# A rank scatter on one core: four-tile loads with four buffers and 9 directly copied tiles, in place of two-tile loads with eight buffers and 11

## The chip, the core and the metric

The kernel runs on one core of one Trainium2 chip. The metric is the device time of one launch in microseconds (us); the other cores do nothing. The core has five engines that run side by side: PE (TensorE, matrix products), DVE (VectorE), ACT (ScalarE), POOL (GpSimd) and SP (SyncE). Data moves by DMA: an engine's instruction stream issues a transfer, and 16 DMA engines, shared by everything the core issues, carry it out. A transfer that covers 128 partitions is cut into packets that are spread evenly over the 16 DMA engines, and each of them adds 1 to the transfer's semaphore when its own share has landed, so a transfer is done when its semaphore has risen by 16.

## The reference

```python
def setup_inputs():
    B, N, D = 8, 2048, 2560
    return {"x": randn(B, N, D) as float32, "scores": randn(B, N) as float32}

def reference(x, scores):
    order = np.argsort(scores, axis=1)
    ranks = np.argsort(order, axis=1)
    out = np.zeros_like(x)
    out[b_idx, ranks, :] = x
    return out
```

In each of 8 batches, row n of `x` (2560 floats, 10 KB) goes to the row of `out` that is the rank of its score among the batch's 2048 scores. So 16384 rows of 10 KB, 167.8 MB, are read once and written once, in an order that depends on the data.

## The kernel before

A tile is 128 rows of one batch (1.31 MB); there are 16 tiles in each batch, 128 in all. Two things go on at once.

**Ranks.** DVE finds the rank of every row. For a batch it first copies all 2048 scores, which PE has spread over the 128 partitions, from PSUM into `s_all` (L235). Then for each tile it counts how many scores are smaller than each of the tile's 128 own scores (the instructions of L258, two counts and one product with the triangular `mask` that settles equal scores inside a group), adds the counts (L284, L290) and turns them into integers (L307). The product is over a whole group of tiles, so its width is 128 times the number of tiles in the group.

**Moving the rows.** `GROUPS` (L56) cuts a batch into groups of tiles. An entry (first row, m, batches) stands for m tiles; in the batches named last it is moved directly, in the others through SBUF. `ORDER` (L57) is the order of groups in a batch; it fixes the order of the ranks and of the transfers.

- *Bulk groups* (list `BULK`, numbered k over all batches) are loaded into one of `NBUF` buffers `xb` by one DMA, `load` (L119 to L125, issued at L122): partition p gets m consecutive rows, m times 10 KB in one piece. Then m indirect DMAs, `scatter` (L358 to L369, issued at L361), each send 128 rows of 10 KB to the rows named by `rank_i`. Load 0 is issued by SP, all other loads and all scatters by POOL, in one ring which each DMA engine works off in order.
- *Direct groups* go from DRAM to DRAM without a buffer. SP and ACT take turns of 16 rows (L326 to L344): they read 16 row addresses from `rows_i` into registers and issue one DMA for each row, split over the 16 DMA engines into packets of 640 bytes. These wait only for the ranks of their own group.

The order of POOL's work is the loop at L373. `LAG` is 2: before step k sends its scatters, POOL waits until the scatters of step k-2 have wholly landed, and issues into their buffer the load of step k+NBUF-2. Then it waits for load k and for the ranks of group k (L381, L382), and issues the scatters of step k. So at the moment at which the wait for the scatters of step k-2 ends, the ring holds exactly the load of step k+NBUF-3 (the one issued a step ago) and, behind it, the scatters of step k-1. At the start POOL issues NBUF-1 loads in a row (L371, L372).

```python
        for k, (b, g) in enumerate(BULK):
            if k >= LAG and k + NBUF - LAG < len(BULK):
                scatters_done(pl, k - LAG)
                load(pl, k + NBUF - LAG, s_load[(k - LAG) % NBUF])
            ... wait for load k and the ranks of (b, g) ...
            for j in range(GROUPS[g][1]):
                scatter(k, j, 0, P, rank_i, s_scat[i][j])
```

Before, the groups are: tile 0 of each batch, direct in all 8 batches; tile 1, direct in batches 0 to 2 and bulk in the others; and seven groups of two tiles, all bulk. That makes 11 direct tiles (1408 rows), and 61 bulk loads: 56 of two tiles and 5 of one, 117 tiles and 117 scatters in all. Eight buffers of 20 KB per partition hold them.

SP and ACT wait for their own row copies at L348; SP waits for the last NBUF steps' scatters at L394.

Of the kernel before, what the change touches and what calls it, by code (L numbers as in the profile page):

```python
# [7 lines left out]
P = 128  # L8
# [32 lines left out]
def kernel(  # L41
# [7 lines left out]
    B, N, D = x.shape  # L49
# [3 lines left out]

    GROUPS = [(0, 1, range(B)), (P, 1, range(3))] + [(256 * i, 2, ()) for i in range(1, 8)]  # L56
    ORDER = [2, 0, 1, 3, 4, 5, 6, 7, 8]  # L57
    MMAX = max(m for _, m, _ in GROUPS)
    MDIR = max([m for _, m, direct in GROUPS if direct], default=1)
    MBULK = max(m for _, m, direct in GROUPS if len(direct) < B)  # L60
    BULK = [(b, g) for b in range(B) for g in ORDER if b not in GROUPS[g][2]]
    DIRECT = [(b, g) for b in range(B) for g in ORDER if b in GROUPS[g][2]]

    SPLIT = ()
    LAST = 2
    NBUF = 8
    LAG = 2
    G = 16

    def first_col(g):  # L70
        return GROUPS[g][0] // P

# [14 lines left out]
    rows_i = [pool.tile([MDIR, P], I32, name=f"rows_i{i}") for i in range(len(DIRECT))]  # L87
    xb = [pool.tile([P, MBULK * D], F32, name=f"x{i}") for i in range(NBUF)]
    ps_col = psum.tile([P, 512], F32, name="ps_col")
# [8 lines left out]
    with tc.tile_critical(no_gpsimd_drain=True):  # L98
# [6 lines left out]
        s_first = nc.alloc_semaphore("first")  # L105
        s_load = [nc.alloc_semaphore(f"load{i}") for i in range(NBUF)]
        s_scat = [
            [nc.alloc_semaphore(f"scat{i}_{j}") for j in range(MBULK)]
            for i in range(NBUF)
        ]  # L110
        s_rows = {sp: nc.alloc_semaphore("rows_sp"), act: nc.alloc_semaphore("rows_act")}
        s_last = [
            [nc.alloc_semaphore(f"last{i}_{j}") for j in range(MBULK)]
            for i in range(NBUF)
        ]
        n_scat = [[0] * MBULK for _ in range(NBUF)]
        n_last = [[0] * MBULK for _ in range(NBUF)]

# [111 lines left out]
        for b in range(B):  # L230
# [11 lines left out]
            dve.after(dve, t_copied)  # L242
            for g in ORDER:
                r, m, _ = GROUPS[g]
# [128 lines left out]
        for k, (b, g) in enumerate(BULK):  # L373
            i = k % NBUF
# [50 lines left out]
```

## Time and profile before

| | |
|---|---|
| median of 3 runs | 795.35 us (795.24, 795.35, 797.09) |
| the profiled execution, its own time | 797.09 us |
| span of its profile, first to last instruction | 795.4 us |
| DVE busy | 411.2 us (52% of the span) |
| POOL busy | 148.4 us (19%) |
| PE busy | 33.3 us (4%) |
| HBM read, written | 167.84 MB, 167.77 MB: 422 GB/s over the span |
| row copies issued by SP and by ACT | 704 each, from 24.3 us to 690.5 us |
| loads issued by POOL | 60, from 2.7 us to 734.9 us |
| scatters issued by POOL | 117, from 17.8 us to 753.1 us |

The profile's times count from the first instruction. Busy time leaves out the issuing of DMAs by SP and ACT and counts POOL's. In the view of stretches each line gives a stretch's ends and length, then for PE, PE's weight load, DVE and POOL the busy time and number of instructions, then the granted PE clock, then the mean busy share of the 16 DMA engines and the GB/s that they moved. A byte copied from DRAM to DRAM counts once in these GB/s, a byte that goes through SBUF twice. In the timeline each line gives start, duration, engine, line, operation, what is written from what, and in brackets how long the engine was idle before and what ended that. The trace also holds every DMA packet with its start, duration, bytes and queue, and every semaphore increment with its time.

### The profile page before, as it was taken

Reading aid. Unit: us, or ns where it says so; the run is one execution under the profiler, and the core shown is the slowest. Engines: PE = TensorE matmul, PEld = TensorE weight load, DVE = VectorE, ACT = ScalarE, POOL = GpSimd, SP = SyncE. Lnnn points to the kernel's source line nnn. Section 1 sums busy time; section 2 is a strip of 40 time slices with the busy share of each in tenths; the row PEclk is TensorE's granted clock in tenths of the full one; section 3 lists DMA queues with packets and bytes.
Section 4 is the critical chain, followed back from the end, with each engine's and each line's share of the span. In section 5 each row is a group of like instructions: output and inputs, shape, how many; then the busy total and the mean of one; then the engine's idle time right before and its main releaser. Section 6 shows DMA issues by size and latency. Waiting matters only on the chain.

```text
span 795.4 us, 4586 instructions
## 1 busy us (share of the span) xinstructions
PE 33.3 (4%) x155; PEld 27.2 (3%) x155; DVE 411.2 (52%) x1002; POOL 148.4 (19%) x186
## 2 busy tenths in 40 slices
PE   3002010020020100200000000000000000000000
PEld 3001010010010100100000000000000000000000
DVE  6999999999999999999994000000000000000000
POOL 3102121212121212022111212122121212111600
PEclk9555555555555555555555555555555555555555
DMA  8999999999999999999999999999999999999994
GB/s 364 431 402 365 424 415 425 417 422 417 425 417 418 347 420 422 422 367 420 421 420 423 397 397 421 420 419 380 420 411 423 420 386 407 401 431 426 390 428 193
DMA packets 70737, 321.57 MB, mean 404 GB/s; under 512 B 25384, under 2 KB 47912, under 8 KB 47912
## 3 DMA queue, kind: packets, MB, share of 16 engines
q0 software_dynamic: 25488, 304.10, 91.3%
q1 hardware_dynamic: 22688, 9.94, 4.9%
q10 hardware_dynamic: 22528, 7.25, 3.9%
q14 instruction: 32, 0.26, 0.1%
q8 instruction: 1, 0.02, 0.0%
HBM read 167.84 MB, written 167.77 MB: 422 GB/s over the span
## 4 chain that ended last, share of the span: by engine, by line
DVE 47%; DMA 40%; issue 4%; POOL 3%; PE 1%; POOLq 0%; SPq 0%
DVE trash L258 41%; DMA out_dram<-x,rank_i 38%; DVE s_all L235 2%; DMA x<-in_x_dram 2%; POOL out_dram L361 2%; DVE rank L284 1%; DVE rank L290 1%; DVE rank_i L307 1%; POOL x L122 1%; DMA s_in<-in_scores_dram 0%; PE ps_all L190 0%; PE ps_col L169 0%; DVE rows_i L220 0%; POOLq L28 0%; DVE s_col L177 0%
## 5 line engine op out<-in xcount | busy, mean ns | idle before, releaser
L258 DVE TENSOR_SCALAR_CACHE_REDUCE trash<-s_all,s_col 128x1792 bf16<-128x1792 f32 (+9 forms) x248 | 315.3, 1306 | 0.3
L122 POOL DMA_DIRECT2D x<-in_x_dram x60 | 33.8, 565 | 545.8 <-DMA out_dram<-x,rank_i 376.5
L361 POOL DMA_INDIRECT out_dram<-x,rank_i x117 | 112.8, 964 | 59.0 <-issue 35.3
L258 DVE SCALAR_TENSOR_TENSOR trash<-s_all,s_col,mask 128x256 bf16<-128x256 f32 (+1 forms) x128 | 59.0, 461 | 0.0
L190 PE MATMUL ps_all<-ident,s_col 128*128 128x128 f32 x128 | 27.2, 399 | 247.4 <-DVE s_all L235 247.0
L190 PEld LDWEIGHTS ps_all<-ident,s_col 128*128 128x128 f32 x128 | 24.4, 213 | 249.4 <-DVE s_all L235 249.0
L235 DVE COPY s_all<-ps_all 128x512 f32<-128x512 f32 x32 | 20.1, 683 | 1.8 <-PE ps_all L190 1.5
L258 DVE DVE_READ_ACCUMULATOR trash<-s_all,s_col 128x1 f32 x248 | 19.9, 80 | 0.0
L290 DVE TENSOR_TENSOR rank<-rank,acc 128x2 f32<-128x2 f32 (+1 forms) x72 | 11.5, 160 | 2.5
L284 DVE TENSOR_TENSOR rank<-acc,acc 128x2 f32<-128x2 f32 (+1 forms) x72 | 11.5, 160 | 2.5
L307 DVE CAST rank_i<-rank 128x2 int32<-128x2 f32 (+1 forms) x61 | 10.7, 176 | 1.8
L258 DVE DVE_READ_ACCUMULATOR trash<-s_all,s_col,mask 128x1 f32 x128 | 10.2, 80 | 0.0
L300 PE MATMUL ps_row<-ident,rank 128*1 128x128 f32 x11 | 4.1, 372 | 101.3 <-DVE rank L290 92.7
L300 PEld LDWEIGHTS ps_row<-ident,rank 128*1 128x1 f32 x11 | 0.9, 79 | 105.0 <-DVE rank L290 95.5
L220 DVE TENSOR_SCALAR rows_i<-ps_row 1x128 int32<-1x128 f32 x11 | 3.0, 272 | 0.0
L177 DVE COPY s_col<-ps_col 128x128 f32<-128x128 f32 x1 | 0.3, 292 | 4.8 <-PE ps_col L169 4.8
L169 PE MATMUL ps_col<-ident,s_in 8*128 8x8 f32 x16 | 2.0, 261 | 4.0 <-DMA s_in<-in_scores_dram 4.0
L169 PEld LDWEIGHTS ps_col<-ident,s_in 8*128 8x128 f32 x16 | 1.9, 211 | 4.0 <-DMA s_in<-in_scores_dram 4.0
L150 POOL TENSOR_SCALAR_AFFINE_SELECT mask<-mask 128x256 f32<-128x256 f32 x2 | 0.8, 398 | 0.0
L162 DVE MEMSET acc<- 128x128 f32 x1 | 0.2, 165 | 1.1 <-SPq L98 1.1
L133 POOL MEMSET mask<- 128x512 f32 x1 | 0.5, 525 | 0.0
L132 POOL MEMSET ident<- 128x128 f32 x1 | 0.2, 204 | 0.5 <-SPq L98 0.5
(5 smaller groups left out, 0.7 us busy)
## 6 DMA issues: line engine op xcount, KB each, us to landing
x<-in_x_dram POOLq DMA_DIRECT2D x55, 2560.0 KB, 19.2
out_dram<-in_x_dram SPq DMA_DIRECT2D x704, 10.0 KB
out_dram<-in_x_dram ACTq DMA_DIRECT2D x704, 10.0 KB
x<-in_x_dram POOLq DMA_DIRECT2D x5, 1280.0 KB, 16.7
x<-in_x_dram SPq DMA_DIRECT2D x1, 2560.0 KB, 13.4
out_dram<-x,rank_i POOLq DMA_INDIRECT x117, 23.5
s_in<-in_scores_dram SPq DMA_DIRECT2D x1, 64.0 KB
```

The lines of the kernel that those rows point to most:

```text
L122: line.eng.dma_start(out=xb[k % NBUF][:, :m * D], in_=x[b, r:r + P * m, :].rearrange("(p j) d -> p (j d)", j=m),).then_inc(sem, 16)
L150: nc.gpsimd.affine_select(out=part, in_=part, pattern=[[0, MMAX], [-1, P]], compare_op=OP.is_ge, fill=0.0, base=-half, channel_multiplier=1,)
L169: nc.tensor.transpose(out=ps_col[:, B * c:B * (c + 1)], in_=s_in[:, r + j:r + m * P:m], identity=ident[:B, :B],)
L190: nc.tensor.transpose(out=ps_all[:, P * c:P * (c + 1)], in_=s_col[:, c, b:b + 1].to_broadcast([P, P]), identity=ident[:],)
L220: nc.vector.tensor_scalar(out=rows_i[DIRECT.index((b, g))][:m, :], in0=ps_row[:m, :P], scalar1=float(b * N), scalar2=float(ROW), op0=OP.ad ...
L235: nc.vector.tensor_copy(out=s_all[:, 512 * q:512 * (q + 1)], in_=ps_all[:, 512 * q:512 * (q + 1)],)
L258: how.pop("do")(out=trash[i][:, :P * (hi_c - lo_c)], in0=s_all[:, P * lo_c:P * hi_c], accum_out=acc[which][:, col:col + 1], **how,)
L284: nc.vector.tensor_tensor(out=rank[:, cols], in0=acc[0][:, cols], in1=acc[1][:, cols], op=OP.add)
L290: nc.vector.tensor_tensor(out=rank[:, cols], in0=rank[:, cols], in1=acc[2][:, cols], op=OP.add)
L300: nc.tensor.transpose(out=ps_row[:m, :P], in_=rank[:, cols], identity=ident[:])
L307: nc.vector.tensor_copy(out=rank_i[:, cols], in_=rank[:, cols])
L361: nc.gpsimd.indirect_dma_start(out=out_flat, out_offset=bass.IndirectOffsetOnAxis(ap=index[:hi - lo, col:col + 1], axis=0), in_=xb[k % NBU ...
```

## The change

```diff
-    GROUPS = [(0, 1, range(B)), (P, 1, range(3))] + [(256 * i, 2, ()) for i in range(1, 8)]
-    ORDER = [2, 0, 1, 3, 4, 5, 6, 7, 8]
+    GROUPS = [(0, 1, range(B)), (P, 1, range(1))] + [(256 + 512 * i, 4, ()) for i in range(3)] + [(1792, 2, ())]
+    ORDER = [2, 0, 1, 3, 4, 5]
...
-    NBUF = 8
+    NBUF = 4
```

Tile 1 of a batch is now direct in batch 0 alone, so 9 tiles (1152 rows) are copied directly and 119 go through SBUF. The other 14 tiles of a batch are three groups of four tiles and one of two. That makes 39 bulk loads: 24 of four tiles (40 KB per partition, 5.2 MB), 8 of two and 7 of one. There are four buffers of 40 KB per partition, the same 160 KB as before. `MMAX` rises from 2 to 4, so `mask` is twice as wide and the products with it in a group of four tiles cover 512 columns. Everything else follows from these three constants: POOL issues 38 loads and 119 scatters, three loads ahead at the start instead of seven, and at step k the load of step k+2 instead of k+6; SP and ACT copy 576 rows each. The order in a batch is: four tiles, one (tile 1, where it is bulk), four, four, two. Who issues what, and the waits, stay as they are.

## Prediction

> **What bounds the kernel now.** I read the page's slices and queues first.
>
> ```profile
> DMA  8999999999999999999999999999999999999994
> ...
> q0 software_dynamic: 25488, 304.10, 91.3%
> q1 hardware_dynamic: 22688, 9.94, 4.9%
> q10 hardware_dynamic: 22528, 7.25, 3.9%
> ```
>
> The DMA engines are busy in every slice but the first and last, and POOL's ring (q0) takes nine tenths of their time; q1 (SP) and q10 (ACT) are the row copies. No compute engine is near. So the time is the bill of packets, plus whatever holds the engines up. The stretches show where that is:
>
> ```profile
> 10.00:46.00 36.00, 2.71 (x18) 1.88 (x18) 35.44 (x86) 3.90 (x4) 0.58 1.01 431
> 66.00:80.00 14.00, 1.25 (x5) 0.26 (x3) 13.76 (x33) 3.31 (x4) 0.62 1.03 343
> 100.00:250.00 150.00, 12.38 (x52) 10.14 (x52) 147.43 (x358) 28.78 (x35) 0.51 1.02 420
> 262.00:275.00 13.00, 3.18 (x15) 3.18 (x16) 12.72 (x33) 4.21 (x6) 0.50 1.03 308
> 340.00:352.00 12.00, 0.00 (x0) 0.00 (x0) 11.79 (x31) 3.21 (x5) 0.50 1.04 345
> 740.00:780.00 40.00, 0.00 (x0) 0.00 (x0) 0.00 (x0) 9.10 (x10) 0.50 1.01 417
> 786.00:791.00 5.00, 0.00 (x0) 0.00 (x0) 0.00 (x0) 0.00 (x0) 0.50 0.06 25
> ```
>
> Steady work moves 420 GB/s; at 66, 262 and 340 us it falls to 343, 308 and 345 while the busy share stays above 1. There the ring has run dry on some engines, which do row copies alone, or the packets take longer. And the last line: 0.06 is one sixteenth. In the last 5 us one DMA engine works alone. The semaphore increments say the same: the 16 engines' shares of one DMA land 1.5 us apart in the first loads, 4 to 5 us at 100 us, up to 9.3 us at 350 us, and the last scatter 7 us apart. So the end is set by one late engine; what the other 15 lose costs nothing unless it slows that one. POOL's timeline shows why the ring runs dry:
>
> ```profile
> 31.32 0.95 POOL L361 DMA_INDIRECT out_dram<-x,rank_i  x1 [0.30 <-issue]
> 63.73 0.57 POOL L122 DMA_DIRECT2D x<-in_x_dram  x1 [31.46 <-DMA out_dram<-x,rank_i]
> ...
> 70.42 0.56 POOL L122 DMA_DIRECT2D x<-in_x_dram  x1 [3.58 <-DMA out_dram<-x,rank_i]
> ...
> 87.49 0.57 POOL L122 DMA_DIRECT2D x<-in_x_dram  x1 [13.98 <-DVE rank L284]
> ...
> 261.90 0.57 POOL L122 DMA_DIRECT2D x<-in_x_dram  x1 [10.49 <-DMA out_dram<-x,rank_i]
> ...
> 272.58 0.56 POOL L122 DMA_DIRECT2D x<-in_x_dram  x1 [7.58 <-DMA out_dram<-x,rank_i]
> ...
> 287.48 0.56 POOL L122 DMA_DIRECT2D x<-in_x_dram  x1 [11.81 <-DVE trash L258]
> ```
>
> At 63.73 step 2 gets past the wait for step 0's scatters, and only step 1's two scatters are left in the ring (two tiles, 6.2 us), less what the quick engines have already done. The load issued at 261.90 starts its first packet at 265.5, 3.6 us after its issue. So if the late engine has less than its lag plus 3.6 us queued when POOL wakes, quick engines run dry. (The 13.98 us named after DVE end when step 2's scatters have landed, at 86.9; DVE is ahead of POOL by then.)
>
> **The bill of packets.** In the trace's packet records the usual durations are 0.385 us for 10 KB, 0.761 for 20 KB, 0.032 for 640 bytes and 0.009 for a semaphore packet; the next packet starts 0.004 (after the semaphore one 0.003) before the last ends, so the spacings are 0.381, 0.757, 0.028 and 0.006. 10 KB more cost 0.376, so I estimate a 40 KB packet, which this trace does not hold, at 0.757 + 0.752 = 1.509; bounds: 0.757 twice (1.514) and four times 0.376 (1.504), half a us either way over the 192 on an engine. Each engine carries 8 packets and one semaphore packet of every load and scatter, and one 640-byte and one semaphore packet of every row.
>
> Before, per engine: 448 x 0.757 = 339.1 and 40 x 0.381 = 15.2 for loads, 936 x 0.381 = 356.6 for scatters, 177 x 0.006 = 1.1, rows 1408 x 0.034 = 47.9; sum 759.9. After: 192 x 1.509 = 289.7, 64 x 0.757 = 48.4, 56 x 0.381 = 21.3, scatters 952 x 0.381 = 362.7, 157 x 0.006 = 0.9, rows 1152 x 0.034 = 39.2; sum 762.2. **Term 1: +2.3 us**: the two tiles cost more through SBUF than directly, and longer packets save little.
>
> **What the late engine loses besides.** From its first load packet (2.5 us) to its last landing (790.9) are 788.4 us, 28.5 above the bill. Taking each DMA's last increment minus that of the DMA before, less its bill and 0.034 us for each packet of the ring (one packet of q1 and one of q10 are served between two of q0): load 8, issued at 63.73, takes 10.42 us where 6.36 are due, 4.1 lost; load 7, 1.2. Ten steps in batches 3 to 7 meet a one-tile group, so only three tiles' worth (9.2 us) is queued at the wake; loads around them lose 1.8 (load 23), 0.7 (load 28) and 0.3 to 0.6 several times, together about 5, so 0.5 each. About 3.5 are lost in five lumps of 0.7 at instruction fetches (8 KB packets on another queue). Scatter packets of the late engine are lengthened to about 0.41: 450 such records, 12.0 us above 0.385. 2.7 stay unassigned.
>
> **What the change does to these.** *Start.* Step 2 now wakes with step 1's four scatters queued, 12.4 us against a need of 3.6 plus some 5 of lag: the 4.1 of load 8 go. Does the first scatter come in time? The 14 tiles loaded ahead take 14 x 8 x 0.3765 = 42 us from 2.5, so until 46 with rows. DVE has four tiles' ranks at about 23.5 (10.58, then 3.1 a tile from its timeline, plus 0.26 for each 512-wide product, estimated from 0.346 at 128 and 0.477 at 256 columns); load 0, on SP's queue, has 12 us of packets and shares engines with POOL's loads, landing by 27 at the latest. Step 1's ranks come at about 44, before its scatters are due at 59. **Term 2: -4.1.** If that cover is gone (a load 0 20 us late), DMA idles for what is missing.
>
> *Wakes with little queued.* The groups run 4, 1, 4, 4, 2. At step k the ring holds load k+1 and scatters k-1: in tiles 3, 8, 5, 6, 8 through a batch. Only the first step of batches 1 to 7 has three. Ten such wakes become seven; everything else has more than before. At 0.5 each: 3.5 in place of 5. **Term 3: -1.5**; bounds for one wake: 0 (load 31 lost nothing) and 4.1 (load 8). I take the mean of the ten, which have the same three tiles queued.
>
> *Fetches* scale with the unrolled rows, 18% fewer: **term 4: -0.6.** *Lengthened scatter packets:* they come only while rows are copied (none after 700.2 us). The share of scatter packets in the ring's rises from 16/27 to 32/45, rows fall to 1152: 834 against 819 of them meet rows. Nothing; bounds -2.2 (18%, if the rows cause them) and +0.2.
>
> *Costed at nothing.* DVE: 96 products wider, +25 us, 24 fewer group endings of 0.5, so it ends near 430 instead of 415, while batch b's ranks are due at some 99 x b. POOL's wider mask (memset 0.53, selects 2 x 0.40, doubled) delays its first load by 1.3 us behind load 0's 12. Rows: 576 of a queue take two turns each, 1152 of the ring's 1413, so they end near 650 and SP's last waits follow as before; at three turns each (1728) they would become the end. The tail after the last landing stays 4.5 us.
>
> The sum: 2.3 - 4.1 - 1.5 - 0.6 = -3.9. The profiled execution (797.09, of it 795.4 span) would become 793.2; the median of the runs, 1.7 below it, 795.35 - 3.9 = **791.4**.
>
> **Two rules.** The Trainium skill (DMA: Bandwidth & Descriptors, Anatomy of one DMA) adds about 2.0 us to each DMA beside its bytes; 22 fewer loads would save 44 us if they ran one by one, giving 751. Here the trace disagrees: behind a DMA's semaphore packet the next one's data follows after 0.006 us. The same page (Latency and other measured facts) guesses that slow DMA engines suffer from the descriptor ring's port; with 11% fewer ring packets (1593 to 1413) that would be an estimated 1.3 of the 12.0 us, 790.1. The scatter-only stretch from 740 us, all ring and no rows, has none of it, which speaks against.
>
> **Rivals.** *The wakes become the bound (slower).* Place: step 4, 9, ... 34, where POOL waits for a four-tile scatter and quick engines sit dry, then all read a 5.2 MB load in step. Price per wake p: the total is -7.4 + 7p, so it decides from p = 1.06. With load 23's 1.8: +5.2, 800.6. For: loads read in step after a dry moment took 1 to 2 us per 20 KB packet. Against: nine of ten such wakes cost under 0.8. *No change:* load 8's 4.1 come from the start of scatters under row copies, not from the short ring, and return: +0.2, 795.6. For: load 7 lost 1.2 with a full ring. Against: the dip to 343 GB/s comes 3 us after the wake. *More gained:* long runs of one kind of packet free the late engine of its lengthened ones: -3.9 - 12.0, 779.5; nothing but the two pure stretches speaks for it.
>
> **How the numbers follow.** Forecast 0.46, no change 0.25, slower 0.23, more gained 0.06. The runs can't tell less than 0.3% (2.4 us) from nothing. The forecast and the large gain give faster 0.52. p = 0 gives 788.0, the low end; the high end, 798, takes in the no-change case and p up to 1.4. The likeliest one's own range is 788 to 793.
>
> **What would show it.** Packets of 40 KB at 1.51 us; load 4 (issued near 60 us) in 12.4 us on the late engine; seven dips a hundred us apart; row copies ended near 650; one engine last at the end. Wrong if 40 KB packets run over 1.55, if DMA idles before 60 us, or if rows run past 780.

## The result, and the profile after

The changed kernel takes 803.49 us (median of 4 runs, 802.98 to 804.12); the kernel before, in the same comparison, 795.91. The ratio is 1.0094 (95% interval 1.0076 to 1.0111): 7.6 us slower, where 3.9 us faster was forecast. The span of the profile grew from 795.4 to 801.9 us, by 6.5; the profiled run of before was the longest of its four, hence the difference.

The page of the changed kernel, slices and queues:

```profile
DMA  9999999999999999999999999999999999989993
...
q0 software_dynamic: 22608, 306.72, 90.7%
q1 hardware_dynamic: 18592, 11.24, 5.1%
q10 hardware_dynamic: 18432, 5.94, 3.1%
```

The DMA engines are as full as before, with POOL's ring at nine tenths. The stretches of the changed kernel (columns as in the view of before), the first where load 8 had cost the kernel before its dip, the next in steady work, four around the wakes with three tiles queued, and the end:

```profile
66.00:80.00 14.00, 2.06 (x10) 1.65 (x8) 13.86 (x32) 5.16 (x6) 0.62 1.05 437
100.00:200.00 100.00, 8.09 (x34) 6.71 (x34) 98.86 (x216) 17.92 (x20) 0.52 1.02 421
206.00:220.00 14.00, 0.00 (x0) 0.00 (x0) 13.90 (x32) 5.44 (x7) 0.50 1.06 256
310.00:324.00 14.00, 0.00 (x0) 0.00 (x0) 13.86 (x32) 4.01 (x5) 0.50 1.05 425
611.00:625.00 14.00, 0.00 (x0) 0.00 (x0) 0.00 (x0) 5.92 (x7) 0.50 1.04 388
712.00:724.00 12.00, 0.00 (x0) 0.00 (x0) 0.00 (x0) 3.96 (x5) 0.50 0.98 385
789.00:794.00 5.00, 0.00 (x0) 0.00 (x0) 0.00 (x0) 0.00 (x0) 0.50 0.15 66
795.50:801.90 6.40, 0.00 (x0) 0.00 (x0) 0.00 (x0) 0.00 (x0) 0.50 0.00 0
```

The dip at 66 us is gone (437 GB/s against 343), as forecast. There are new ones at three of the four wakes with three tiles queued, down to 256 GB/s; the one at 310 us moves 425. One late engine still ends the transfers (0.15 is mostly one sixteenth in a stretch that begins with several). The last line is the surprise: after the last landing, at 794.7 us, the core does nothing that the profile counts for 7.2 us. Before, it was 4.1 us (from the last semaphore increment at 791.3; the prediction's 790.9 and 4.5 count from the end of the last data packet). The waits of SP's queue say for what, in the kernel before

```profile
SPq L420 <- PEq L420: 3.3, 2, 2.9
```

and in the changed one

```profile
SPq L420 <- PEq L420: 6.4, 2, 6.0
```

(line waited at, releaser, us in total, times, longest us). This is the barrier at the end of the program. PE is only the last to report; the instruction records, which the page doesn't count as busy, show that all engines wait for one instruction of POOL, a drain:

```
kernel    start us  duration us  engine  instruction
before      791.64        3.015  POOL    DRAIN
changed     795.08        6.112  POOL    DRAIN
```

So the sum comes out as follows, with the bill recomputed from the counted packets by the spacings of the prediction, and the late engine's loss as what its last landing lies above the bill:

| | before | changed | difference |
|---|---|---|---|
| first load packet, us | 2.6 | 2.5 | -0.1 |
| bill of packets | 759.9 | 762.3 | +2.4 |
| loss of the late DMA engine | 28.7 | 29.8 | +1.1 |
| last landing at | 791.3 | 794.7 | +3.4 |
| from there to the end of the span | 4.1 | 7.2 | +3.1 |

These differences add up to the 6.5 us of the span. The prediction had +2.3 for the bill, -6.2 for the late engine's loss (terms 2 to 4) and nothing for what follows the last landing.

### The profile page after: what moved, and what is told of

The parts are those of the page before. It is cut to its first block, busy times and chain, and to the rows that moved or that the text cites. A ratio compares the mean times of both kernels' runs of the same rounds, so it can differ in the third digit from the quotient of the medians.

```text
span 801.9 us, 3940 instructions
## 1 busy us (share of the span) xinstructions
PE 33.0 (4%) x153; PEld 27.3 (3%) x153; DVE 425.9 (53%) x930; POOL 141.5 (18%) x166
## 4 chain that ended last, share of the span: by engine, by line
DMA 73%; issue 12%; POOL 10%; POOLq 0%; SPq 0%
DMA out_dram<-x,rank_i 68%; POOL out_dram L361 9%; DMA x<-in_x_dram 6%; POOL x L122 1%; POOLq L28 0%; SPq L128 0%; SPq L420 0%; SPq L98 0%
## 5 line engine op out<-in xcount | busy, mean ns | idle before, releaser
L258 DVE TENSOR_SCALAR_CACHE_REDUCE trash<-s_all,s_col 128x768 bf16<-128x768 f32 (+6 forms) x248 | 315.1, 1305 | 0.3
L361 POOL DMA_INDIRECT out_dram<-x,rank_i x119 | 117.2, 985 | 80.4 <-issue 36.5
L122 POOL DMA_DIRECT2D x<-in_x_dram x38 | 21.5, 567 | 543.9 <-DMA out_dram<-x,rank_i 354.2
L258 DVE SCALAR_TENSOR_TENSOR trash<-s_all,s_col,mask 128x512 bf16<-128x512 f32 (+2 forms) x128 | 84.6, 661 | 0.0
L290 DVE TENSOR_TENSOR rank<-rank,acc 128x4 f32<-128x4 f32 (+2 forms) x48 | 7.8, 162 | 1.7
L284 DVE TENSOR_TENSOR rank<-acc,acc 128x4 f32<-128x4 f32 (+2 forms) x48 | 7.8, 162 | 1.7
L307 DVE CAST rank_i<-rank 128x4 int32<-128x4 f32 (+2 forms) x39 | 7.1, 182 | 1.1
## 6 DMA issues: line engine op xcount, KB each, us to landing
x<-in_x_dram POOLq DMA_DIRECT2D x7, 1280.0 KB, 29.5
```

The costliest lines, as they stand in the source:

```text
L122: line.eng.dma_start(out=xb[k % NBUF][:, :m * D], in_=x[b, r:r + P * m, :].rearrange("(p j) d -> p (j d)", j=m),).then_inc(sem, 16)
L258: how.pop("do")(out=trash[i][:, :P * (hi_c - lo_c)], in0=s_all[:, P * lo_c:P * hi_c], accum_out=acc[which][:, col:col + 1], **how,)
L284: nc.vector.tensor_tensor(out=rank[:, cols], in0=acc[0][:, cols], in1=acc[1][:, cols], op=OP.add)
L290: nc.vector.tensor_tensor(out=rank[:, cols], in0=rank[:, cols], in1=acc[2][:, cols], op=OP.add)
L307: nc.vector.tensor_copy(out=rank_i[:, cols], in_=rank[:, cols])
L361: nc.gpsimd.indirect_dma_start(out=out_flat, out_offset=bass.IndirectOffsetOnAxis(ap=index[:hi - lo, col:col + 1], axis=0), in_=xb[k % NBU ...
```

## The experiments

All runs are listed here first; each is told below. "Landing" is the last semaphore increment in the profile, "drain" POOL's last drain (where an explicit one was added, the number is the time from the last landing to the end of that one). There is one profile for each kernel, so the last four columns come from a single execution. Ratios are against the kernel before on the same chip.

| kernel | median us | ratio (95% interval) | bill | late engine's loss | landing | drain |
|---|---|---|---|---|---|---|
| before | | | 759.9 | 28.7 | 791.3 | 3.0 |
| changed | 803.49 | 1.0094 (1.0076 to 1.0111) | 762.3 | 29.8 | 794.7 | 6.1 |
| e1: two-tile loads, 9 direct | 799.89 | 1.0061 (1.0048 to 1.0075) | 763.4 | 25.4 | 791.4 | 6.7 |
| e2: four-tile loads, 11 direct | 807.07 | 1.0153 (1.0139 to 1.0167) | 758.8 | see text | 798.9 | 5.6 |
| e3: changed, other order | 800.04 | 1.0061 (1.0047 to 1.0074) | 762.3 | 25.7 | 790.5 | 7.7 |
| e4: e2, other order | 807.60 | 1.0155 (1.0141 to 1.0169) | 758.8 | see text | 798.9 | 6.1 |
| e5: before, LAG 3 | 796.89 | 1.0011 (1.0002 to 1.0019) | 759.9 | 28.1 | 790.6 | 3.1 |
| e6: changed, 20 small loads | 810.94 | 1.0187 (1.0174 to 1.0201) | 762.5 | 38.0 | 803.0 | 5.6 |
| e7: before, 4 small loads | 799.44 | 1.0042 (1.0029 to 1.0055) | 760.0 | 29.6 | 792.1 | 3.0 |
| e8: changed, POOL waits | 803.62 | 1.0101 (1.0087 to 1.0116) | 762.3 | 29.8 | 794.7 | 6.1 |
| e9: changed, early drain | 800.79 | 1.0067 (1.0054 to 1.0081) | 762.3 | 29.5 | 794.5 | 3.1 |
| e10: before, early drain | 794.23 | 0.9976 (0.9967 to 0.9985) | 759.9 | 28.4 | 790.9 | 1.5 |
| e11: two-tile loads, 10 direct | 799.60 | 1.0046 (1.0032 to 1.0060) | 761.7 | 28.5 | 792.7 | 4.9 |
| e12: two-tile loads, 12 direct | 801.36 | 1.0066 (1.0052 to 1.0080) | 758.2 | 29.2 | 789.9 | 8.6 |
| e13: two-tile loads, none direct | 816.63 | 1.0203 (1.0153 to 1.0253) | 778.9 | 21.6 | 803.0 | 8.3 |
| e14: four-tile loads, none direct | 801.15 | 1.0064 (1.0051 to 1.0077) | 777.4 | 13.7 | 793.5 | 5.4 |
| e15: two-tile loads, 8 direct | 809.71 | 1.0176 (1.0160 to 1.0191) | 765.2 | 31.2 | 798.9 | 7.6 |

### The two halves of the change: e1 and e2

e1 is the kernel before with nine direct tiles:

```diff
-    GROUPS = [(0, 1, range(B)), (P, 1, range(3))] + ...
+    GROUPS = [(0, 1, range(B)), (P, 1, range(1))] + ...
```

> The first half of the change alone: two-tile loads and eight buffers as before, but 9 directly copied tiles instead of 11. Bill per DMA engine by the spacings of the prediction: 339.1 + 21.3 + 362.7 + 1.1 + 39.2 = 763.4, 3.5 above the kernel before; 14 steps instead of 10 meet a one-tile group. Theory A (the change lost because wakes with three tiles queued are dear, 1.3 us each after four-tile groups, and the bill): bill +3.5, four more wakes at the 0.5 of the kernel before +2, fewer fetches -0.6: about 5 us slower than before (800 to 801). Theory B (the 40 KB packets or four-tile steps as such slow the late engine, wakes don't matter): only the bill and the fetches, +3 (798 to 799). Last drain of POOL: 3 us as before if it goes with the four-tile groups or the order, 6 if with the number of bulk tiles.

It is 4.5 us slower than the kernel before (799.89 against 795.38 in that comparison), between the two theories and for the reason of neither. Its last landing is at 791.4, 0.1 after that of before, although its bill is 3.5 higher and more steps meet a one-tile group; why its late engine lost 3.3 us less is open. In the profiles the whole difference lies behind the landing, in a drain of 6.7 us.

e2 is the changed kernel with eleven direct tiles (`range(1)` back to `range(3)`).

> The other half alone: four-tile loads and four buffers as in the changed kernel, but 11 directly copied tiles as before. Bill 289.7 + 48.4 + 15.2 + 356.6 + 0.9 + 47.9 = 758.7, 3.5 below the changed kernel and 1.2 below before. Wakes with three tiles queued: 5 (first steps of batches 3 to 7) instead of 7. Theory A: -3.5 - 2 x 1.3 + 0.6 against the changed kernel, 797 to 798. Theory B: -3.5 + 0.6, about 800 to 801.

807.07 us, outside both expectations. Both had forgotten what the prediction itself used: on each engine a row is two packets of its queue, and in the packet records one packet of that queue stands between two of POOL's ring (a turn). 704 rows of a queue need 1408 turns, and this ring has 1377 packets on each engine. The rows can't be done in time. Two stretches of e2:

```profile
784.00:790.00 6.00, 0.00 (x0) 0.00 (x0) 0.00 (x0) 0.00 (x0) 0.50 0.16 39
791.00:796.00 5.00, 0.00 (x0) 0.00 (x0) 0.00 (x0) 0.00 (x0) 0.50 0.06 3
```

From 791 us one engine works alone and moves 3 GB/s: row packets. The ring's last packet ends at 789.8, the last row packet starts at 795.7, and the last landing is at 798.9. So with four-tile loads 11 direct tiles are too many, because fewer, longer packets leave fewer turns; the two halves of the change belong together.

### Do wakes with little queued cost time? e3, e4, e5

e3 and e4 move the one-tile group so that no wake finds fewer than five tiles queued, in the changed kernel and in e2:

```diff
-    ORDER = [2, 0, 1, 3, 4, 5]
+    ORDER = [2, 0, 3, 4, 1, 5]
```

> The changed kernel with the groups of a batch in the order 4, 4, 4, 1, 2 tiles instead of 4, 1, 4, 4, 2 (the one-tile group follows the third four-tile group). Then no wake finds fewer than five tiles queued; the bill, the rows and the loads are the same. Theory A: the 9.1 us that loads 6, 11, 16, 21, 26, 31 and 36 lost fall to 1 or 2: 795 to 797 and no dips to 310 to 390 GB/s. Theory B: no change, 802 to 805, whatever the dips do.

> Four-tile loads, four buffers, 11 direct tiles and the order 4, 4, 4, 1, 2 (4, 4, 4, 2 where tile 1 is direct). No wake with fewer than five tiles queued, and the bill is 758.7. Theory A: 803.5 - 3.5 + 0.6 - 8 = 792 to 793, faster than both. Theory B: 800 to 801, like the same without the new order.

e3 comes to 800.04 us, 3.5 less than the changed kernel. Its stretches where the changed kernel had its wakes:

```profile
206.00:220.00 14.00, 0.00 (x0) 0.00 (x0) 13.79 (x35) 4.67 (x4) 0.50 0.97 403
310.00:324.00 14.00, 0.00 (x0) 0.00 (x0) 13.79 (x35) 0.95 (x1) 0.50 1.03 433
611.00:625.00 14.00, 0.00 (x0) 0.00 (x0) 0.00 (x0) 0.95 (x1) 0.50 1.07 452
712.00:724.00 12.00, 0.00 (x0) 0.00 (x0) 0.00 (x0) 1.15 (x2) 0.50 0.96 416
```

256 GB/s has become 403, 388 has become 452, 385 has become 416, and the last landing comes 4.2 us earlier (790.5). So the wakes do cost the changed kernel time, about half of what theory A said; the drain took 1.6 us back (7.7 against 6.1). e4's time says nothing on the wakes: like e2 it ends with row packets (the last one at 795.8). But its ring's last packet ends at 785.5, 4.3 us before that of e2, which agrees with e3.

e5 asks the same of the kernel before, with a deeper queue:

```diff
-    LAG = 2
+    LAG = 3
```

> The kernel before with LAG 3 instead of 2: a step waits for the scatters of the step three back, so eight tiles instead of four are queued in the ring at a wake (at least seven where a one-tile group is near), and loads are issued one step later, with five instead of six ahead. Same packets. Theory A (wakes with little queued cost the late engine time): load 8 loses nothing (-4) and loads 23, 28, 37, 52, 55 little (-3 or more); last landing at 784 to 787 instead of 791.3, 788 to 791 us in all. Theory B (these losses come from the start of scatters under row copies and from fetches): last landing at 790 to 792, time as before. POOL's last drain (3.0 us before) stays, since the number of transfers in the ring is the same.

```profile
66.00:80.00 14.00, 1.22 (x5) 0.23 (x3) 13.76 (x33) 5.32 (x7) 0.50 1.03 425
262.00:275.00 13.00, 3.15 (x15) 3.15 (x16) 12.72 (x33) 2.48 (x3) 0.50 1.03 421
340.00:352.00 12.00, 0.00 (x0) 0.00 (x0) 11.79 (x31) 2.49 (x3) 0.50 1.03 423
786.00:791.00 5.00, 0.00 (x0) 0.00 (x0) 0.00 (x0) 0.00 (x0) 0.50 0.05 23
```

All three dips of the kernel before (343, 308 and 345 GB/s) are gone, and the time is not better (ratio 1.0011, 1.0002 to 1.0019). The last line shows what stays: one engine still ends the work alone, at nearly the same time (790.6 against 791.3). The other 15 now run up to 21 us ahead of it instead of 9, and wait longer at the end. Added up over its DMAs against the bill without rows, the late engine's loads cost 7.3 us less (22.4 above that bill against 29.7; load 8 loses nothing) and its scatters 7.1 more (51.6 against 44.5). Two executions with the same transfers (the changed kernel and e8, or the kernel before and e10) differ by up to 2 us in such a sum, so the shift of 7 is real. What it no longer lost at one place it lost at another. That disproves the theory of the prediction for this kernel: here the losses read off single DMAs were not terms that can be taken away one by one. In e3 they partly were: the same sum over its loads fell from 19.2 us in the changed kernel to about 15, and that over its scatters stayed within 1 us (nine last increments of e3 are missing from the trace and are set by the bill). Why the late engine gave the time back in e5 and kept it in e3 is open.

### POOL's last drain: e6 to e12 and e15

Does the drain go with the number of transfers that the ring has taken? e6 and e7 add loads of 4 bytes a partition:

```diff
         for k in range(1, NBUF):
             load(pl, k, s_load[k])
+        for i in range(20):          (4 in e7)
+            nc.gpsimd.dma_start(out=small[:, i:i + 1], in_=x[0, 0:P, i:i + 1]
+            ).then_inc(s_small, 16)
+        sp.wait(s_small, 320)        (64 in e7)
```

> The changed kernel plus 20 loads of 4 bytes per partition issued by POOL behind the first loads, so that POOL issues 177 transfers and each DMA engine's ring takes 1593 packets, as in the kernel before. It asks what sets POOL's last drain, 3.0 us before, 6.1 after, 5.6 to 7.7 in the four kernels tried. Theory C (it goes with the number of transfers or packets that the ring has taken): drain 3.0, time 803.5 - 3 + 20 x 9 packets of some 0.02 to 0.06 us (4 to 10) = 804 to 810. Theory D (it goes with the groups, the order or the last steps): drain stays at 6.1, time 807 to 813.

> The kernel before plus 4 loads of 4 bytes per partition issued by POOL behind the first loads: 181 transfers and 1629 packets per ring, as in the kernel with two-tile loads and 9 direct tiles, whose drain was 6.7 us. Theory C: drain 6.7, time 795.4 + 3.7 + 1 to 2 = 800 to 801. Theory D: drain 3.0, 796 to 797.5.

The small loads took two ring packets each, not nine, so the packet counts meant in the expectations weren't reached (1453 and 1601); the transfer counts were. 177 transfers gave 5.6 us in e6 and 3.0 in the kernel before; 181 gave 3.0 in e7 and 6.7 in e1. So in these profiles the number of transfers is not what sets it. (e7's profile is of an execution of 797.89 us; its others took up to 800.17, and their drains are not known.) e6's 20 small loads also delayed its landing by 8.3 us.

e8 lets POOL itself wait for the last scatters (`scatters_done(pl, k)` for `scatters_done(sp, k)` in the last loop).

> The changed kernel with POOL instead of SP waiting for the last scatters. Nothing in the ring changes. If POOL's last drain does work that has been open since its last issue and that POOL can do while it waits, the drain shrinks to under 1 us and the time to 797 to 798; if it is work of the drain itself, 6.1 us and 803 to 804 stay.

803.62 us, drain 6.1 to the hundredth: waiting does none of its work. That the length is a property of the kernel rather than chance is supported by this repeat and by the kernel before, e5 and e7 (3.02, 3.10 and 3.02).

e9 and e10 put a drain right behind POOL's last scatter:

```diff
                 else:
                     scatter(k, j, 0, P, rank_i, s_scat[i][j])
+        nc.gpsimd.drain()
```

> The changed kernel with an explicit drain on POOL right after its last scatter is issued, while the DMA engines still have some 29 us of work. Theory E (POOL's last drain is work of POOL that can be done before the last landing): this drain takes it on, the last one shrinks to well under 1 us, time 803.5 - 6 = 797 to 798, so that about 3 us of the change's loss are shown to be the drain. Theory F (the last drain's length is set at the end of the program, whatever came before): 6 us stay at the end, 803 to 804.

> The same explicit drain in the kernel before. Theory E: its last drain of 3.0 us shrinks to well under 1, 792 to 793, a version faster than before. With both drains gone the two kernels differ by the last landing alone, 3.4 us in the profiles (up to 5). Theory F: 795 to 796.

Both gain, and less than theory E had it. The changed kernel goes from 803.49 to 800.79 us, the kernel before from 796.10 to 794.23 (ratio 0.9976, 0.9967 to 0.9985): a version that is faster than both. In the view of SP's waits the barrier is now held up by POOL's queue for 1.1 us in e10 instead of the 2.9 above, and for 2.6 instead of 6.0 in e9:

```profile
SPq L98 <- POOLq L98: 1.1, 1, 1.1
```

```profile
SPq L98 <- POOLq L98: 2.6, 1, 2.6
```

The early drain runs through the rest of the transfers and ends 1.5 us (e10) and 3.1 us (e9) after the last landing. So of 3.0 and 6.1 us about half stays behind the last landing when the drain is issued early, in both kernels. That the other half was work done while transfers still ran is the simplest reading; it was not tried otherwise.

e11, e12 and e15 are two-tile kernels with 10, 12 and 8 direct tiles (`range(2)`, `range(4)` and `()` for the second group).

> Two-tile loads, eight buffers, 10 direct tiles: between the kernel before (11, drain 3.0 us) and the one with 9 (drain 6.7). Bill 339.1 + 18.3 + 359.7 + 1.1 + 43.5 = 761.7. Theory C' (the drain goes with the number of transfers or bulk tiles): a drain between 3.0 and 6.7, time 797 to 798.5. Otherwise 3.0 or less and 795.5 to 796.5, or 6 and more and 799 to 800.

> Two-tile loads, eight buffers, 12 direct tiles. Bill 339.1 + 12.2 + 353.5 + 1.1 + 52.2 = 758.1, 1.8 below before. Its rows need 1536 turns of a ring of 1575 packets, of which some 30 pass before the first row, so rows end within a few us of the scatters: last landing 789 to 792 if they just fit, later by what is left over if they don't. Theory C': drain 3 or less, 793 to 795.5. Otherwise 797 or more.

> Two-tile loads, eight buffers, 8 direct tiles (tile 0 of each batch). With 12, 11, 10 and 9 direct tiles POOL's last drain was 8.6, 3.0, 4.9 and 6.7 us. If it climbs by 1.85 us for each tile more in the ring and falls back at some point (a saw tooth), 8 direct tiles give 8.5 or, past the next fall, 1 to 2. If it goes with the time or the rows in another way, anything else. Bill 339.1 + 24.4 + 365.8 + 1.1 + 34.8 = 765.2; last landing at 792 to 796.

With 12, 11, 10, 9 and 8 direct tiles the drain is 8.6, 3.0, 4.9, 6.7 and 7.6 us. It is neither flat nor one slope: it falls by 5.5 us between 12 and 11 and climbs from there, by 1.9, 1.8 and 0.9. e12 has the earliest last landing of all kernels with rows (789.9; its rows end at 785.2, just in time) and loses it to the longest drain. The kernel before happens to sit at the lowest point of the series. What the drain does in that time was not found; neither the number of transfers nor the packets alone set it (the changed kernel and e3 have the same packets in another order, and 6.1 and 7.7 us).

### Are the row copies what makes one engine late? e13 and e14

e13 and e14 copy nothing directly: eight groups of two tiles with eight buffers, and four groups of four with four buffers.

```diff
-    GROUPS = [(0, 1, range(B)), (P, 1, range(1))] + ...
-    ORDER = [2, 0, 1, 3, 4, 5]
+    GROUPS = [(512 * i, 4, ()) for i in range(4)]
+    ORDER = list(range(4))
```

> Two-tile loads and eight buffers with no directly copied tile at all: eight groups of two in each batch, 128 tiles through SBUF, no row copies. Bill 64 x 8 x 0.757 + 1024 x 0.381 + 191 x 0.006 = 387.6 + 390.1 + 1.1 = 778.8. The late DMA engine lost 25 to 30 us above its bill in every kernel so far, whatever the queueing. Theory G (the row copies lengthen its scatter packets and mix with its loads): without rows it loses under 10, last landing 787 to 791, and the 16 engines land within 2 us of each other. Theory H (it is late whatever runs): loss 25 to 30, last landing 806 to 811. The last drain comes on top, 1 to 8.6 us.

> The same with four-tile loads and four buffers: four groups of four in each batch, no row copies, never fewer than eight tiles queued at a wake. Bill 256 x 1.509 + 390.1 + 159 x 0.006 = 386.3 + 390.1 + 1.0 = 777.4, 1.4 below the two-tile kernel without rows. Theory G: last landing 785 to 790, so a version that may beat the kernel before. Theory H: 804 to 810. If 40 KB packets or four-tile steps cost something of their own, it shows as this kernel being slower than the two-tile one.

In e14 the loss falls to 13.7 us, with a last landing at 793.5; in e13 to 21.6 and 803.0. Both losses are above the 10 us that theory G allowed and below the 25 of theory H. Theory G is right on the scatter packets: lengthened ones (0.395 to 0.5 us) are 13 in e14 and 28 in e13, 0.2 and 0.9 us in all, against 455 and 12.5 us before. It is not the whole story, since an engine is still late, by 10.3 us in e14. There the loss has a clear end in time: summed over its DMAs the late engine lost 11.1 us up to 430 us and 0.1 after, and DVE's last rank is at 437. Its loads carry 9.3 us of the loss, its scatters 1.9. (In e13 it is 15.3 up to 430 us and 4.1 after.) Two stretches of e14:

```profile
100.00:400.00 300.00, 17.95 (x80) 16.20 (x80) 297.19 (x578) 54.64 (x60) 0.56 1.01 428
450.00:750.00 300.00, 0.00 (x0) 0.00 (x0) 0.00 (x0) 56.43 (x64) 0.50 1.01 430
```

The rate is 428 GB/s while DVE is busy and 430 after. That DVE's work is the cause was not tried, and it is not the only thing that ends there: eight of e14's nine instruction fetches during the transfers (0.31 us each, 2.5 us in all) also lie before 430 us. e13's runs scatter from 807.55 to 830.57 us, more than any other kernel's, so its median isn't interpreted, and its landing and loss come from one of these runs (814.07). In e14 four-tile loads after 430 us cost the late engine nothing beyond the bill, so there neither 40 KB packets nor four-tile steps slow it by themselves.

## Why the prediction was wrong, point by point

The step that failed is the subtraction of terms 2, 3 and 4 from the late engine's loss. They were to take 6.2 us off; the loss rose by 1.1 us (28.7 to 29.8), a miss of 7.3 us. The tail behind the last landing, put at no change, adds another 3.1. Together these are the 10.4 us between the forecast of -3.9 and the +6.5 of the spans. The other 1.1 us of the 7.6 in the medians come from comparing medians instead of the two profiled executions.

- *"The tail after the last landing stays 4.5 us."* This is the largest term that was put at nothing: it rose by 3.1 us in the profiles. The trace of before held POOL's drain of 3.0 us, but the prediction took the stretch behind the last landing as fixed. e8 repeats its length, e1 shows that 9 direct tiles instead of 11 are enough to lengthen it, and e9 and e10 that issuing it early takes part of it off the end. What sets its length is open.
- *Term 1, +2.3 for the bill.* Right: +2.4 by the counted packets. The 40 KB packet was estimated at 1.51 us; its median is 1.514.
- *Term 2, -4.1 for the start.* The place was right and the gain did not arrive. Load 4, issued at 63.63, took 12.37 us on the late engine (12.4 forecast), and the dip is gone. But e5 removed the same dip from the kernel before and moved the last landing by only 0.7: there the late engine gave the time back in its scatters (7.1 us). That this happened in the changed kernel too was not tried by itself. (The 3.6 us from the issue at 261.90 to the load's first packet are 3.8 by the packet records.)
- *Term 3, -1.5 for the wakes.* Wrong in sign. The seven loads that follow a wake with three tiles (6, 11, 16, 21, 26, 31, 36) lost 10.8 us, of which rows are 0.31 each, so 8.6 and 1.2 each instead of the 0.5 taken over from two-tile steps, above the 1.06 from which the rival decides. (The kernel before has nine such wakes, not ten: at the tenth, step 55, no load is left to issue. The loads issued at the nine lost 3.4 us together, 0.4 each.) The timeline shows one of the seven:

```profile
205.52 0.56 POOL L122 DMA_DIRECT2D x<-in_x_dram  x1 [24.03 <-DVE trash L258]
206.39 0.97 POOL L361 DMA_INDIRECT out_dram<-x,rank_i  x1 [0.30 <-issue]
207.66 0.95 POOL L361 DMA_INDIRECT out_dram<-x,rank_i  x1 [0.30 <-issue]
208.92 0.95 POOL L361 DMA_INDIRECT out_dram<-x,rank_i  x1 [0.31 <-issue]
210.18 0.95 POOL L361 DMA_INDIRECT out_dram<-x,rank_i  x1 [0.30 <-issue]
215.91 0.56 POOL L122 DMA_DIRECT2D x<-in_x_dram  x1 [4.79 <-DVE trash L258]
```

  POOL wakes at 205.52 with three tiles left for an engine that is 8 us behind; the load issued then is load 11, which lost 2.7 us. By e3 the wakes as a whole are worth 4.2 us of landing, so the rival "the wakes become the bound" named a real cost, but not the whole: with these 8.6 us its sum gives 796.6 us, 7 below the measured time. In time e3 gets back 3.5 of the 7.6 us, a little under half.
- *Lengthened scatter packets: "Nothing".* 500 records and 15.2 us against 455 and 12.5: +2.7 where -2.2 to +0.2 was allowed. That they come almost only with row copies is confirmed by e13 and e14 (28 and 13 records).
- *Term 4, -0.6 for fetches,* was not tested by itself.
- *Costed at nothing:* DVE's end (437.9, forecast near 430; in the kernel before it is at 426, not 415) and POOL's wider mask did no harm. Rows ended at 678.5 instead of near 650, still well before the scatters.
- *The premise.* Terms 2 and 3 rest on reading a loss off one DMA of the late engine and subtracting it from the end. In ten kernels with row copies (both kernels, e5, e7 to e12 and e15) the late engine lost 28.1 to 31.2 us above its bill, with and without dips; e1 and e3 lost 25.4 and 25.7, and e6, with its 20 small loads, 38.0. The bill was the reliable part. The losses above it did not follow a sum over single DMAs. (In e2 and e4 rows end the transfers, so no such loss is given.)

The two rules of the Trainium skill: 22 fewer loads would have saved an estimated 44 us by a fixed 2.0 us for each DMA (DMA: Bandwidth & Descriptors, Anatomy of one DMA); the changed kernel, with these 22 fewer, landed 3.4 us later. No run shows anything like it: in e14 and e13, without rows, 32 fewer loads moved the landing by 9.5. The descriptor ring's port as the cause of slow engines, which the page guesses for engines 7 and 15 (same page, Latency and other measured facts), gets no support from e14: with the ring alone at work after 437 us, the late engine loses nothing. The packet records carry no engine's number, so whether the late engine is one of these two is not known.

## What to carry to other kernels

Where the DMA engines are full, add up the packets of the engine that ends last; dips in the bandwidth of the others may cost nothing, and filling them may gain nothing (0.7 us of landing in e5, but 4.2 in e3). Small packets on other queues live on the turns that a ring's packets leave them, so longer packets mean fewer turns: count both before changing one (1408 turns did not fit beside 1377 packets in e2; 1536 fitted beside 1575 in e12). Look at what stands behind the last landing in the profile before and after, instruction by instruction; a drain there was worth almost as much as the change's whole effect on the transfers, and issuing it earlier took 1.9 us off the kernel before.

## What was not expected of the hardware

- POOL's last drain took 3.0 to 8.6 us in one profile each of kernels of the same kind, the same to 0.1 us where only the waits or LAG were changed. Issued early it still ended 1.5 and 3.1 us after the last landing.
- In every run one of the 16 DMA engines ends last by itself. In the kernel before, 455 of its 936 scatter packets of 10 KB took about 0.41 instead of 0.385 us, all of them while row copies ran; in the kernels without row copies 28 (e13) and 13 (e14) did.
- Without row copies and with four-tile loads its loss over the DMAs fell into the time in which DVE was at work (11.1 us up to 430 us, 0.1 after); with two-tile loads 4.1 of 19.4 us came later.
